# Shared expert blocks summed by twos, shorter scatters, and the last LayerNorm split over three engines, in a two-layer decoder

## The chip, the core and the metric

The kernel runs as one program on one core of a Trainium2 chip. The metric is the device time of a run in microseconds. Five engines work side by side, each in the order of its own queue: TensorE (PE in the profile), VectorE (DVE), ScalarE (ACT), GpSimd (POOL), and SyncE (SP), which here only issues transfers.

## The reference, cut to what matters

Two decoder layers over 512 tokens of 1024 columns, in float32. Each layer is a mixer and then a mixture of 64 experts:

```python
scores = sigmoid(xf @ router_w)
topi = top_k(masked(scores + router_b), 6)
for e, rows in experts:
    hb = silu(xf[rows] @ w_gate[e]) * (xf[rows] @ w_up[e])
    out[rows] += (hb @ w_down[e]) * topw[rows, e]
x = layer_norm(alpha * x + g2 * (out + shared(xf)))
```

Every token goes to 6 of 64 experts, 3072 rows in all, and every expert has 3 MB of weights (w_gate, w_up, w_down, 1 MB each). The second layer's last LayerNorm is the output.

## The kernel before, in words

The 512 tokens lie in four tiles of 128 (`self.x`). The router sorts the experts by their number of tokens, apart from the first two (SINGLE), and the sorted places are laid into **blocks** of 128 rows (`blocks`, L50): 20 lone blocks with one expert each, 14 two-expert blocks of 2 x 64 rows, 4 four-expert blocks of 4 x 32 rows. `share` (L1167) brings the capacities into the slot arithmetic; an expert with more rows than its place sends the rest through the loop in `extra` (L1683, loop at L1690), which stands behind the blocks and runs as many rounds as there are such parts.

`moe` (L1471) runs the 38 blocks (NB) in one loop from L1570. A round b works on three blocks. `widen` (L1327) multiplies block b with w_gate and w_up (L1336) and forms silu times up on ScalarE and VectorE (L1337, L1338). `narrow` (L1351) multiplies block b-1 with w_down (L1369), four experts in two halves with a yield between them. `turn` (L1316) transposes block b+1's gathered rows (L1324), `turn_back` (L1341) transposes block b's result (L1347), and `slots` makes the index lists of later blocks (L1270).

What happens to a block's result depends on its kind. A **lone** block is scaled on VectorE (L1375) and added to rows of a DRAM buffer `acc` by an indirect transfer of GpSimd (L1376), always 128 rows. A **shared** block is split into a high and a low part (yh, yl: L1383 to L1385) and brought back to the tiles by `combine` (L1390): for each of four tiles and two halves of the columns, two products with a one-hot matrix (L1396) into one PSUM buffer and one VectorE addition to `self.x` (L1397). These are eight units a block, four ahead of the next block's transposes and four behind them.

The order of TensorE's work in the loop is the program's (`manual_schedule`). SyncE issues the weight loads in order (L1302): gate and up go round five places (`eslot`, L1399), w_down round a ring of three (`slot`, L199), and the w_down of an expert is issued behind gate and up of the third expert after it (LAG). The PSUM buffers are three for products ("mm"), three for transposes and combines ("tr"), two small ones.

In the last round, `acc` is read back in eight pieces (L1615) and added on VectorE (L1616). Behind the loop the last block's combine and LayerNorm go tile by tile: two units, `ln_stats` (L307) with two statistics passes on VectorE, one aggregate and a root (L239 VectorE, L240 GpSimd), then `ln_next` (L318), two VectorE passes over 1024 columns. In the last layer tile 0 goes to ScalarE and GpSimd instead (`ln_here`, L327). There VectorE and GpSimd follow the order written in the program.

## Time and profile before

| | us |
|---|---|
| runs, median (three: 2149.96 to 2156.48) | 2151.9 |
| the profiled execution, its own time | 2150.13 |
| its span in the profile | 2148.1 |
| TensorE products busy in the span | 1955.6 |
| VectorE busy | 1236.2 |
| ScalarE busy | 508.3 |
| GpSimd busy | 441.2 |
| mean granted TensorE clock, as a share of full speed | 0.967 |

Busy times of engines overlap and don't add up to the span. A matmul's end is modelled, so what counts for TensorE is how far the starts of its instructions lie apart. "Idle before <- X" names what ended an engine's idle time; an engine with q behind it is that engine's instruction queue (waits, branches, issue of transfers).

### The profile page before, as it was taken

The numbers are of one execution on the slowest core, as the hardware profiler recorded it, in microseconds if no ns is written. First come the engines' busy times: TensorE is split into PE (matmuls) and PEld (weight loads), VectorE is DVE, ScalarE is ACT, GpSimd is POOL, SyncE is SP. The second block draws the span as 40 slices with busy tenths as digits, with TensorE's granted clock in tenths as the row PEclk, the third lists the DMA queues.
The fourth block names the chain that finished last, engine by engine and source line by source line (L and its number), as shares of the span: only waits on it lengthen the run. The fifth ranks groups of instructions, "written<-read, shape, count | busy, mean of one in ns | idle before, by whom it ended". The sixth has DMA issues, their size and how long they took to land. (4 is left out here: it accounts for less than half of the span.)

```text
span 2148.1 us, 28655 instructions
## 1 busy us (share of the span) xinstructions
PE 1955.6 (91%) x10619; PEld 1193.5 (56%) x10619; DVE 1236.2 (58%) x3169; ACT 508.3 (24%) x969; POOL 441.2 (21%) x313
## 2 busy tenths in 40 slices
PE   4999878999999999999688999999999999998995
PEld 3777778644443443443567877888443444443432
DVE  6666687844444553542778778578453535544436
ACT  3412533111111111111334455523111111111110
POOL 1222234111010110101034445144211010110102
PEclk9999998999999999999899999999999999999997
DMA  7765455998998989988332111128989989989893
GB/s 296 257 240 186 182 199 195 352 330 325 406 349 351 389 316 361 381 325 300 96 118 59 40 60 60 46 99 309 357 335 365 363 327 402 353 317 405 329 348 126
DMA packets 128679, 572.18 MB, mean 266 GB/s; under 512 B 16943, under 2 KB 54255, under 8 KB 72473
## 3 DMA queue, kind: packets, MB, share of 16 engines
q1 hardware_dynamic: 103600, 499.81, 60.1%
q0 software_dynamic: 19632, 55.79, 9.3%
q10 hardware_dynamic: 5304, 14.72, 1.9%
q8 instruction: 85, 1.39, 0.3%
q14 instruction: 58, 0.47, 0.1%
HBM read 550.33 MB, written 34.61 MB: 272 GB/s over the span
## 5 line engine op out<-in xcount | busy, mean ns | idle before, releaser
L1336 PE MATMUL ps_mm<-wslot,xT 128*64 128x512 f32 (+2 forms) x1216 | 404.5, 596 | 1.1 <-ACT xT L1325 0.8
L1369 PE MATMUL ps_mm<-wslot,hT 128*64 128x512 f32 (+2 forms) x1024 | 329.6, 627 | 20.1 <-DMA wslot<-in_moe_w_down_dram 19.9
L1338 DVE SCALAR_TENSOR_TENSOR hh<-hh,t,ps_mm 128x256 f32<-128x256 f32 x76 | 36.5, 480 | 434.5 <-ACT hh L1337 434.5
L1336 PE MATMUL ps_mm<-parts,xT 128*64 128x512 f32 (+2 forms) x832 | 280.0, 595 | 0.7 <-ACT xT L1325 0.4
L1336 PEld LDWEIGHTS ps_mm<-wslot,xT 128*64 128x64 f32 (+2 forms) x1216 | 142.1, 148 | 218.9 <-issue 205.7
L1369 PEld LDWEIGHTS ps_mm<-wslot,hT 128*64 128x64 f32 (+2 forms) x1024 | 105.5, 152 | 225.1 <-issue 197.5
L232 PE MATMUL ps_mm<-parts,hTh 128*128 128x256 f32 x704 | 206.7, 295 | 14.0 <-DVE op L400 6.9
L1294 POOL DMA_INDIRECT xg<-hd,idx x76 | 86.3, 1136 | 615.1 <-PE ps_tr L1396 525.4
L233 PE MATMUL ps_mm<-parts,hTh 128*128 128x256 f32 x704 | 204.0, 291 | 4.9 <-DVE parts L220 4.2
L234 PE MATMUL ps_mm<-parts,hTl 128*128 128x256 f32 x704 | 203.3, 291 | 0.0
L225 POOL TENSOR_TENSOR parts<-wslot,parts 128x512 fp32r<-128x512 f32 (+1 forms) x79 | 140.6, 1807 | 241.9 <-ACT parts L218 241.8
L1397 DVE TENSOR_TENSOR x<-x,ps_tr 128x512 f32<-128x512 f32 x288 | 183.6, 680 | 11.1 <-PE ps_tr L1396 10.4
L1337 ACT ACTIVATE hh<-ps_mm 128x256 f32<-128x256 f32 x76 | 29.2, 384 | 613.7 <-PE ps_mm L1336 613.7
L1376 POOL DMA_INDIRECT acc<-yh,row x40 | 64.8, 1620 | 498.9 <-DVE yh L1375 498.9
L1336 PEld LDWEIGHTS ps_mm<-parts,xT 128*64 128x64 f32 (+2 forms) x832 | 93.7, 144 | 130.5 <-issue 122.9
L1396 PE MATMUL ps_tr<-yh,ohs 128*128 128x512 f32 x288 | 137.4, 477 | 26.1 <-DVEq L1690 14.0
L232 PEld LDWEIGHTS ps_mm<-parts,hTh 128*128 128x128 f32 x704 | 137.3, 195 | 17.7 <-DVE op L400 4.6
L1325 ACT ACTIVATE xT<-ps_tr 128x512 f32<-128x512 f32 x152 | 84.0, 597 | 245.0 <-PE ps_tr L1324 245.0
L233 PEld LDWEIGHTS ps_mm<-parts,hTh 128*128 128x128 f32 x704 | 137.4, 195 | 6.8 <-DVE parts L220 4.8
L234 PEld LDWEIGHTS ps_mm<-parts,hTl 128*128 128x128 f32 x704 | 136.8, 195 | 2.2 <-issue 0.9
L234 PE MATMUL ps_mm<-hTh,parts 128*128 128x512 f32 (+1 forms) x296 | 120.6, 407 | 9.1 <-POOL parts L225 9.1
L232 PE MATMUL ps_mm<-hTh,parts 128*128 128x512 f32 (+1 forms) x296 | 123.7, 418 | 5.1 <-ACT parts L218 2.5
(456 smaller groups left out, 3124.3 us busy)
## 6 DMA issues: line engine op xcount, KB each, us to landing
wslot<-in_moe_w_down_dram SPq DMA_DIRECT2D x128, 1024.0 KB, 10.4
wslot<-in_moe_w_gate_dram SPq DMA_DIRECT2D x76, 1024.0 KB, 8.2
wslot<-in_moe_w_up_dram SPq DMA_DIRECT2D x76, 1024.0 KB, 11.7
parts<-in_moe_w_gate_dram SPq DMA_DIRECT2D x52, 1024.0 KB, 10.3
parts<-in_moe_w_up_dram SPq DMA_DIRECT2D x52, 1024.0 KB, 8.8
wslot<-in_ada_w_dram SPq DMA_DIRECT2D x44, 1024.0 KB, 5.6
wslot<-in_od_w_in_dram SPq DMA_DIRECT2D x16, 1024.0 KB, 6.2
wslot<-in_ev_w_in_dram SPq DMA_DIRECT2D x12, 1024.0 KB, 6.4
```

What stands on the lines that cost most here:

```text
L225: eng.tensor_sub(lo[:, ks], v[:, ks], hi[:, ks].bitcast(F32))
L232: self.nc.tensor.matmul(out, ah, bh, start=(i == 0), stop=False)
L233: self.nc.tensor.matmul(out, ah, bl, start=False, stop=False)
L234: self.nc.tensor.matmul(out, al, bh, start=False, stop=(i == n - 1))
L1294: self.nc.gpsimd.indirect_dma_start(out=xg, out_offset=None, in_=M["hd"], in_offset=bass.IndirectOffsetOnAxis(ap=idx, axis=0), bounds_chec ...
L1325: nc.scalar.activation(xT[:, 4 * g:4 * g + 4], pt.rearrange("p (k c) -> p k c", k=4), AF.Copy)
L1336: nc.tensor.matmul(pv[a:a + n], xT[:, i, a:a + n], w[0][:, :, i], start=(i == 0), stop=(i == KT - 1))
L1338: nc.vector.scalar_tensor_tensor(h, h, G["wt"], pg[:, FE:], op0=OP.mult, op1=OP.mult)
L1369: nc.tensor.matmul(py[a:a + n], hT[:, k, a:a + n], w[1][:, k, 512 * h:512 * h + 512], start=(k == 0), stop=(k == 1))
L1376: nc.gpsimd.indirect_dma_start(out=M["acc"], out_offset=bass.IndirectOffsetOnAxis(ap=G["tok"], axis=0), in_=yf, in_offset=None, bounds_che ...
L1396: nc.tensor.matmul(po, G["oh"][:, t], y[:, cs], start=(i + k == 0), stop=(i == len(Gs) - 1 and k == 1))
L1397: nc.vector.tensor_add(self.x[t][:, cs], self.x[t][:, cs], po)
```

## The change

Nine edits go together:

- `width`: lone places 9 to 13 get a capacity of 96 rows, 14 to 19 of 80 (128 before), and the scatter of L1376 carries only so many rows. The products keep 128 rows.
- `blocks`: lone and shared blocks are spread in another order; the last three blocks are a four-expert and two two-expert ones, where a lone one stood among them before.
- A lone block's scaled result has a buffer of its own (`ys`, one) and no longer shares the two of the shared blocks' high part; `hh` has one buffer in place of two.
- Shared blocks are combined by twos: the units of a pair make four products into one PSUM buffer and one addition. The last two shared blocks stay single.
- Behind a four-expert block the second half of `narrow` comes at the end of the round, behind the next transposes; the combine of a pair that ends with such a block comes a round later.
- `acc` is read into the three gather buffers, tiles 0 and 1 in round NB-3, 2 and 3 in round NB-2, and added on GpSimd a round later.
- LayerNorm behind the loop: the statistics of tiles 1 and 3 are made on ScalarE in two passes (`ln_stats_act`), one for the sum and one for the squares about the mean. This holds for both layers.
- In the last layer ScalarE and GpSimd also take the first half of tile 1's columns (`norm2`), and the order is written anew.
- In the first layer's output projection the closing step of a group of adaLN sums is no longer put off (`fill`).

```diff
@@ -47,6 +47,11 @@
 ALONE = SINGLE + FULL
 
 
+def width(k):
+
+    return P if k < SINGLE + 7 else 96 if k < SINGLE + 12 else 80
+
+
 def blocks():
 
 
@@ -62,10 +67,10 @@
         a, b = iter(out), iter(more)
         return [next(b if k in at else a) for k in range(n)]
 
-    alone = [((k, 0, P),) for k in range(ALONE)]
+    alone = [((k, 0, width(k)),) for k in range(ALONE)]
     twos = shared(ALONE, TWOS, 2)
     fours = shared(ALONE + TWOS, E - ALONE - TWOS, 4)
-    return alone[:SINGLE] + spread(spread(twos, fours), alone[SINGLE:], 0, 1)
+    return alone[:SINGLE] + spread(spread(twos, fours), alone[SINGLE:], 0.5, 3)
 
 
 BLOCKS = blocks()
@@ -314,6 +319,17 @@
         nc.vector.bn_aggr(mv[:, 0:2], st.rearrange("p a b -> p (a b)"))
         self.rsqrt(mv[:, 2:3], mv[:, 1:2], 1.0, LN_EPS)
         return mv
+
+    def ln_stats_act(self, x, scratch):
+
+        nc = self.nc
+        mv = self.small.tile([P, 4], F32, tag="mv", name="mv", bufs=4)
+        sm = self.small.tile([P, 3], F32, tag="lnsum", name="lnsum", bufs=2)
+        nc.scalar.activation(scratch, x, AF.Copy, accum_out=sm[:, 0:1])
+        nc.scalar.activation(sm[:, 2:3], sm[:, 0:1], AF.Copy, scale=-1.0 / D)
+        nc.scalar.activation(mv[:, 0:1], sm[:, 0:1], AF.Copy, scale=1.0 / D)
+        nc.scalar.activation(scratch, x, AF.Square, bias=sm[:, 2:3], accum_out=sm[:, 1:2])
+        return mv, lambda: self.rsqrt(mv[:, 2:3], sm[:, 1:2], 1.0 / D, LN_EPS)
 
     def ln_next(self, x, mv, rows, h):
 
@@ -1169,7 +1185,12 @@
         nc = self.nc
         cnt, posm = M["count"], M["posm"]
         of = {k: (a, n) for b in BLOCKS for k, a, n in b}
-        runs, k = [], ALONE
+        runs, k = [], SINGLE
+        for n in sorted({width(k) for k in range(SINGLE, ALONE)}, reverse=True):
+            m = sum(width(j) == n for j in range(SINGLE, ALONE))
+            if n < P:
+                runs.append((k, k + m))
+            k += m
         for n, m in ((TWOS, 2), (E - ALONE - TWOS, 4)):
             for j in range(m):
                 runs.append((k, k + n // m))
@@ -1329,7 +1350,7 @@
-        h = G["h"] = M["pool"].tile([P, FE], F32, tag="hh", name="hh", bufs=2)
+        h = G["h"] = M["pool"].tile([P, FE], F32, tag="hh", name="hh", bufs=1)
@@ -1351,9 +1372,9 @@
     def narrow(self, M, G):
 
         nc, hT, pool = self.nc, G["hT"], M["pool"]
-        one = G.get("one")
+        one = G.get("one", 0)
         if one:
-            (yh,) = [pool.tile([P, D], FR, tag="yh", name="yh", bufs=2)]
+            yf = pool.tile([P, D], F32, tag="ys", name="ys", bufs=1)
         elif "y" not in G:
             G["y"] = [pool.tile([P, D], FR, tag=n, name=n, bufs=2) for n in ("yh", "yl")]
             G["oh"] = pool.tile([P, TT, P], FR, tag="ohs", name="ohs", bufs=2)
@@ -1369,12 +1390,11 @@
         if one:
-            yf = yh.bitcast(F32)
             for h, py in enumerate(pys):
                 cs = slice(512 * h, 512 * h + 512)
                 nc.vector.tensor_mul(yf[:, cs], py, M["grow"][:, cs])
-            nc.gpsimd.indirect_dma_start(out=M["acc"], out_offset=bass.IndirectOffsetOnAxis(ap=G["tok"], axis=0),
-                                         in_=yf, in_offset=None, bounds_check=S + P - 1, compute_op=OP.add)
+            nc.gpsimd.indirect_dma_start(out=M["acc"], out_offset=bass.IndirectOffsetOnAxis(ap=G["tok"][:one], axis=0),
+                                         in_=yf[:one], in_offset=None, bounds_check=S + P - 1, compute_op=OP.add)
             yield
             return
         for h, py in enumerate(pys):
@@ -1509,7 +1529,7 @@
                 w = [[] for _ in es]
-                W.append([(a, n, x) for (_, a, n), x in zip(b, w)])
+                W.append([(a, n if len(b) > 1 else P, x) for (_, a, n), x in zip(b, w)])
@@ -1552,7 +1572,9 @@
         self.hes.close()
         with ExitStack() as es:
             M["pool"] = self.pool(f"exp{l}", ctx=es)
-            todo, units = [], []
+            todo, late, shared = [], [], 0
+            nshared = sum(len(b) > 1 for b in BLOCKS)
+            back = {NB - 3: ((), (0, 1)), NB - 2: ((0, 1), (2, 3)), NB - 1: ((2, 3), ())}
 
             for _ in range(NXG - SINGLE):
                 merge((slots(), 2))
@@ -1575,45 +1597,49 @@
                         row.append(self.narrow(M, G[b - 1]))
                         if not G[b - 1]["one"]:
                             todo.append(G[b - 1])
+                            shared += 1
                     if b < NB:
                         fetch(sum(2 * len(x) for x in BLOCKS[:b + LEAD]) + 2)
-                        G[b]["w"], G[b]["one"] = W[b], len(W[b]) == 1
+                        G[b]["w"], G[b]["one"] = W[b], len(W[b]) == 1 and BLOCKS[b][0][2]
                         row.append(self.widen(M, G[b]))
-                    if not todo:
+                    four = b > 0 and len(BLOCKS[b - 1]) > 2
+                    full = len(todo) == 2 or (todo and shared > nshared - 2)
+                    if not full and not four:
                         row.reverse()
                     for x in row:
                         next(x)
-                    for x in row:
+                    for x in row[four:]:
                         for _ in x:
                             pass
-                    if todo and b < NB:
-                        units = [lambda g=todo, t=t, h=h: self.combine(g, t, h) for t in range(TT) for h in range(2)]
+                    units, late = late, []
+                    if full and b < NB:
+                        late = [lambda g=todo, t=t, h=h: self.combine(g, t, h) for t in range(TT) for h in range(2)]
                         todo = []
+                        if not four:
+                            units, late = units + late, []
                     for u in units[:4]:
                         u()
                     if b + 1 < NB:
                         ahead()
-                    if b < NB and not units:
+                    if b < NB and not units and not four:
                         self.turn_back(M, G[b])
                     if b + 1 < NB:
                         self.turn(M, G[b + 1])
-                    if b < NB and units:
+                    if b < NB and (units or four):
                         self.turn_back(M, G[b])
                     next(sl, None)
                     for u in units[4:]:
                         u()
-                    units = []
                     if b == NB - 3 and pre:
                         pre(False)
                     if b == NB - 1 and pre:
                         pre(True)
-                    if b == NB - 1:
-                        for t in range(TT):
-                            for h in range(2):
-                                cs = slice(512 * h, 512 * h + 512)
-                                y = self.wk("acc")
-                                nc.gpsimd.dma_start(y, M["acc"][t * P:(t + 1) * P, cs])
-                                nc.vector.tensor_add(self.x[t][:, cs], self.x[t][:, cs], y)
+                    if NB - 3 <= b < NB:
+
+                        for t in back[b][0]:
+                            nc.gpsimd.tensor_add(self.x[t], self.x[t], M["xg"][(NB - 3 + t) % 3])
+                        for t in back[b][1]:
+                            nc.gpsimd.dma_start(M["xg"][(NB - 3 + t) % 3], M["acc"][t * P:(t + 1) * P])
                     if b == NB - 8:
                         wds = [wd[:, 1], wd[:, 0]]
                         new = lambda n: wds.pop()
@@ -1627,6 +1653,9 @@
                             nc.vector.tensor_mul(wd[:, k], wd[:, k], grow)
                     if 8 <= b < 24 and b % 2 == 0:
                         self.shared_end((b - 8) // 4, b // 2 % 2, parts, wd)
+                    for x in row[:four]:
+                        for _ in x:
+                            pass
             units = [lambda g=todo, t=t, h=h: self.combine(g, t, h) for t in range(TT) for h in range(2)]
             self.extra(M, l)
             M["h"], M["mv"] = M["xg"] + [M["tb"].bitcast(F32)], []
@@ -1635,33 +1664,75 @@
                 for u in units[2 * t:2 * t + 2]:
                     u()
 
+            mv, then = M["mv"], {}
+
             def stats(t):
-                M["mv"].append(self.ln_stats(self.x[t]))
-
-            mv = M["mv"]
+
+                if t % 2:
+                    m, then[t] = self.ln_stats_act(self.x[t], M["h"][t])
+                else:
+                    m = self.ln_stats(self.x[t])
+                mv.append(m)
 
             def store(t, cs):
                 nc.sync.dma_start(self.d["out"][0][t * P:(t + 1) * P, cs], self.x[t][:, cs])
 
+            def norm(t, cs=slice(0, D)):
+                to = M["h"] if nxt else self.x
+                self.ln_next(self.x[t][:, cs], mv[t], [r[:, cs] for r in M["rows"]], to[t][:, cs])
+                if not nxt:
+                    store(t, cs)
+
+            def norm2(t, cs):
+                x = self.x[t][:, cs]
+                nc.scalar.activation(x, x, AF.Identity, bias=mv[t][:, 3:4], scale=mv[t][:, 2:3])
+                yield
+                for op, r in zip((nc.gpsimd.tensor_mul, nc.gpsimd.tensor_add), M["rows"]):
+                    op(x, x, r[:, cs])
+                    yield
+                store(t, cs)
+                yield
+
+            lo, hi = slice(0, D // 2), slice(D // 2, D)
             with self.tc.manual_schedule(engines={mybir.EngineType.DVE, mybir.EngineType.Pool}):
-                for t in range(TT):
-                    sums(t)
-                    if nxt and t:
-                        self.ln_next(self.x[t - 1], mv[t - 1], M["rows"], M["h"][t - 1])
-                    stats(t)
-                    if not nxt and t == 0:
-                        self.ln_shift(mv[0])
-                        self.ln_here(self.x[0], mv[0], M["rows"], nc.gpsimd, nc.gpsimd)
-                        store(0, slice(0, D))
+                sums(0)
+                stats(0)
                 if nxt:
-                    self.ln_next(self.x[3], mv[3], M["rows"], M["h"][3])
+                    sums(1)
+                    stats(1)
+                    norm(0)
+                    then[1]()
+                    sums(2)
+                    norm(1)
+                    stats(2)
+                    sums(3)
+                    stats(3)
+                    norm(2)
+                    then[3]()
+                    norm(3)
                 else:
-                    for t in range(1, TT):
-                        x, n = self.x[t], D // 2 if t == 3 else D
-                        for k in range(0, D, n):
-                            cs = slice(k, k + n)
-                            self.ln_next(x[:, cs], mv[t], [r[:, cs] for r in M["rows"]], x[:, cs])
-                            store(t, cs)
+                    self.ln_shift(mv[0])
+                    g0, g1 = norm2(0, slice(0, D)), norm2(1, lo)
+                    next(g0)
+                    next(g0)
+                    sums(1)
+                    stats(1)
+                    sums(2)
+                    stats(2)
+                    next(g0)
+                    next(g0)
+                    sums(3)
+                    stats(3)
+                    then[1]()
+                    self.ln_shift(mv[1])
+                    next(g1)
+                    norm(2)
+                    then[3]()
+                    for _ in g1:
+                        pass
+                    norm(1, hi)
+                    norm(3, lo)
+                    norm(3, hi)
 
     def moe_end(self, l, xd, early, then):
 
@@ -1786,7 +1857,7 @@
 
             left = [0]
 
-            def fill(n=3):
+            def fill(n=3, wait=True):
 
                 n, left[0] = n + left[0], 0
                 for i in range(n):
@@ -1795,7 +1866,7 @@
                             return
                         l, g = todo.pop(0)
                         queue.extend(self.ada_slabs(l, g, t4, self.mod_end(l, g)))
-                    if i and len(queue) == 1:
+                    if wait and i and len(queue) == 1:
                         left[0] = n - i
                         return
                     queue.pop(0)()
@@ -1808,7 +1879,7 @@
             self.row(grow, self.mod[:, 0, 2])
             rows = self.rows_next(new, 0, 0, (self.mod[:, 0, 3], self.mod[:, 0, 4]))
             wr = self.router(0, new)
-            self.out_project(mixed, d["ev_w_out"][0], grow, d["x"][0], fill, (0, 1, 4, 5, 6, 7, 2, 3))
+            self.out_project(mixed, d["ev_w_out"][0], grow, d["x"][0], lambda: fill(3, False), (0, 1, 4, 5, 6, 7, 2, 3))
             while todo or queue:
                 fill(1)
             hT = self.moe_in(0, new, rows, wr)
```

## Rows read from the trace of the kernel before

**Rows 1.** The page, busy tenths of TensorE in 40 slices of 53.7 us.

```profile
PE   4999878999999999999688999999999999998995
```

**Rows 2.** Windows: stretch, us; busy us (instructions) of each engine, clock, DMA share, GB/s.

```profile
1496.00:2117.00 621.00, 597.30 (x2474) 269.35 (x2474) 287.98 (x850) 79.96 (x152) 80.37 (x63) 0.99 0.92 349
...
1650.00:1700.00 50.00, 49.14 (x212) 21.84 (x209) 26.21 (x84) 6.62 (x13) 6.69 (x6) 1.00 1.00 390
1850.00:1900.00 50.00, 49.18 (x199) 22.14 (x196) 24.12 (x75) 6.98 (x13) 6.39 (x5) 0.97 0.85 311
...
982.00:988.80 6.80, 5.99 (x14) 1.28 (x14) 0.69 (x1) 0.63 (x1) 0.00 (x0) 0.50 1.01 429
```

**Rows 3.** Waits of TensorE over the span: us in total, times, longest.

```profile
PE ps_mm L1369 <- DMA wslot<-in_moe_w_down_dram: 19.9, 8, 4.2
PE ps_tr L1396 <- DVEq L1690: 14.0, 2, 8.0
```

**Rows 4.** Timeline of TensorE, one combine in the second layer: start, us, what.

```profile
2037.45 0.79 PE L1396 MATMUL ps_tr<-yh,ohs 128*128 128x512 f32 x1
...
2040.20 1.31 PE L1324 MATMUL ps_tr<-call,xg 128*128 128x128 f32 x8
...
2041.78 0.47 PE L1396 MATMUL ps_tr<-yh,ohs 128*128 128x512 f32 x1
...
2042.33 0.39 PE L1396 MATMUL ps_tr<-yh,ohs 128*128 128x512 f32 x1
2042.56 0.40 PE L1396 MATMUL ps_tr<-yl,ohs 128*128 128x512 f32 x1
...
2043.93 0.62 PE L1336 MATMUL ps_mm<-wslot,xT 128*32 128x512 f32 x2
```

**Rows 5.** Lines by form, VectorE: count, busy us, mean ns, idle before.

```profile
L1397 DVE TENSOR_TENSOR x<-x,ps_tr 128x512 f32<-128x512 f32 x288 | 183.6, 680 | 11.1 <-PE ps_tr L1396 10.4
```

**Rows 6.** Timeline of TensorE, a combine behind a four-expert block and the products after it.

```profile
2078.87 0.50 PE L1396 MATMUL ps_tr<-yh,ohs 128*128 128x512 f32 x1
...
2082.39 1.31 PE L1324 MATMUL ps_tr<-call,xg 128*128 128x128 f32 x8
...
2086.03 7.09 PE L1336 MATMUL ps_mm<-wslot,xT 128*64 128x512 f32 x32
```

**Rows 7.** Waits of SyncE's queue over the span.

```profile
SPq L1302 <- PE ps_mm L1369: 237.8, 40, 12.5
```

**Rows 8.** Transfers: packets, MB, share of 16 engines; issues, us to landing.

```profile
q0 software_dynamic: 19632, 55.79, 9.3%
...
wslot<-in_moe_w_down_dram SPq DMA_DIRECT2D x128, 1024.0 KB, 10.4
...
acc<-yh,row POOLq DMA_INDIRECT x40, 10.8
```

**Rows 9.** Timeline of the second layer's hand-over.

```profile
2114.40 3.09 DVE L1616 TENSOR_TENSOR x<-x,acc 128x512 f32<-128x512 f32 x5
...
2121.26 0.68 DVE L1383 TENSOR_TENSOR y<-ps_mm,grow 128x512 f32<-128x512 f32 x1
...
2123.06 0.79 PE L1396 MATMUL ps_tr<-yh,ohs 128*128 128x512 f32 x1 [6.01 <-DVEq L1690]
```

**Rows 10.** Timeline of the last LayerNorm.

```profile
2125.96 1.28 DVE L312 BATCH_NORM_STATS2 bn<-x 128x6 f32<-128x512 f32 x2
...
2128.56 1.24 ACT L329 ACTIVATE x<-x,mv 128x1024 f32<-128x1024 f32 x1 [5.19 <-DVE mv L325]
...
2129.88 2.38 POOL L330 TENSOR_TENSOR x<-x,wd 128x1024 f32<-128x1024 f32 x1 [1.55 <-ACT x L329]
...
2144.37 0.75 DVE L322 SCALAR_TENSOR_TENSOR x<-x,mv,wd 128x512 f32<-128x512 f32 x1
```

**Rows 11.** Lines by form, ScalarE's read-out and GpSimd beside VectorE's LayerNorm.

```profile
L649 ACT ACTIVATION_READ_ACCUMULATOR sq<-mixed 128x1 f32 x48 | 9.4, 196 | 0.0
...
L1458 POOL TENSOR_TENSOR h<-h,lnrow 128x1024 f32<-128x1024 f32 x2 | 6.5, 3258 | 0.2
```

## The prediction

> **What bounds the kernel now.** I read the 40 slices first. TensorE's digits [rows 1] show two long plateaus of 8 and 9, slices 8 to 19 and 28 to 39: the expert loops of the two layers. The change touches these, the hand-over after each loop, and the last LayerNorm, so I asked for the stretches [rows 2]. The second layer's loop (1496 to 2117) keeps TensorE 597.3 us busy out of 621; the first layer's is like it. There is little idle time to remove there, so a gain has to come out of time that counts as busy. The transfers are nearly as full: 0.92 of the sixteen DMA engines over the loop, 1.00 in one 50 us stretch, 0.85 in another. Of the twelve such stretches from 1500 to 2100, four stand at 0.99 or more and the others between 0.85 and 0.94 (one of the full and the emptiest stand in the rows). So the loop has two limits a few per cent apart, TensorE first.
>
> The waits of TensorE [rows 3] name two that the change aims at: 19.9 us in eight waits for a w_down load, one per four-expert block, and 14.0 us in two waits at the loop of `extra` (L1690), one per layer.
>
> The timeline of one combine [rows 4] shows what the wait list hides. A product with the one-hot matrix follows the next after 0.23 us where nothing holds it (2042.33 to 2042.56). The eight of the first half take 2.75 us (2037.45 to 2040.20), the eight of the second 2.15 (2041.78 to 2043.93): 4.90 us for 16, where 16 x 0.23 is 3.68. Two products (0.46 us) feed one VectorE addition of 0.68 us [rows 5], and three PSUM buffers can't hide that: VectorE sets the pace. Behind a four-expert block it is worse, 3.52 us for the first half [rows 6], as it also waits for the evacuation just made.
>
> **The change, part by part.**
>
> *Shared blocks summed by twos.* Four products now feed one addition: 0.92 us of TensorE against 0.68 of VectorE, so TensorE sets the pace. A pair costs 32 x 0.23 = 7.4 us, some 7.6 with the starts, for two blocks. Of a layer's 18 shared blocks the first 16 go in pairs (12 two-expert, 4 four-expert ones), the last two singly as now. Before: 12 x 4.90 + 4 x 5.67 = 81.5 us; after: 8 x 7.6 = 60.8. That frees **20.7 us of TensorE per layer**. The 64 additions that go from each layer (43 us of VectorE) lie beside other work and count nothing by themselves.
>
> *The second half of a four-expert block's down product moves behind the transposes.* Its fourth w_down load can't start before the first half has freed a place in the ring of three. The move puts the next block's transposes, the turn back and the slot products in between, 1.6 us where they run now (2040.20 to 2041.78 [rows 4]), some 2 with the wait for the turned block's gate on VectorE. Eight waits of 2.5 us on average lose about 2 each: **7.5 us per layer**, 2.5 us left over. What is late next: this half now frees its own ring places 2 us later, and SyncE, which issues every weight load in order, already waits 237.8 us in 40 waits for exactly that line [rows 7]. So the w_down loads of the blocks behind a four start later.
>
> *What the transfers allow.* TensorE could go 28 us faster per layer, 2.3 us in each 50 us stretch. In the eight stretches with room it can have that (18.7 us); in the four full ones it can have only what the transfers give up. They give up something: the 20 scatters of a layer carry 128 rows now, and after the change 9 x 128 + 5 x 96 + 6 x 80 = 2112 instead of 2560. The software queue takes 9.3% of 2148 us [rows 8] for two layers of gathers (3072 rows each), scatters and 640 cleared rows: 200 us over 12544 rows, 16 ns a row, so 448 rows are 7.1 us per layer, 2.3 of them in the full stretches. Upper end: 21 us per layer. Lower end: nothing, if every us saved turns into a later weight wait, as the ring and the five gate/up places can't carry a lead from an empty stretch over to a full one. No row decides between the ends: the mean fill of 0.92 speaks for the upper one, SyncE's waits for ring places [rows 7] for the lower one. I take half: **10.5 us per layer, 21 for both**.
>
> *The order of lone and shared blocks.* Lone blocks bring 3 MB per 10 us of products, shared ones 6 MB per 10 us; the order changes from near-strict alternation to one with two pairs of neighbouring lone blocks, and ends four, two, two. The weights in total are the same. I cost it at nothing; its cover is the lead of the gate/up loads, and without it the two blocks behind a four pay, which is the third rival below. A lone block's result now has one buffer: the next lone block's multiplication must wait for the scatter, whose landing takes 10.8 us [rows 8]. Neighbouring lone blocks are about 12 us apart, so VectorE may wait a us or two, covered by the next block's gate and up products, 7.1 us [rows 6].
>
> *The read-back of the scattered rows* leaves VectorE. Before, its eight additions stand in VectorE's queue ahead of the last block's evacuation [rows 9]: after the last down products TensorE idles 6.01 us, until the combine starts at 2123.06. The multiplication at L1383 that ends this takes 0.68 us, and TensorE starts 1.1 us after it (2121.94 to 2123.06). Without the additions 1.8 us of the 6.0 are left: 4.2 gained; of the first layer's 8.0, 6.2. **10.4 us.** GpSimd now makes four additions of 1024 columns, 2.38 us each by its multiplication of that shape [rows 10]; the first two fall under the last blocks, the last two need the last combine of their tile and end beside the last down products and their evacuation. Cost zero to 2 us; zero taken, since tiles 2 and 3 are summed last.
>
> *The last LayerNorm.* VectorE runs nearly without gaps from the first addition to the end (2144.37 + 0.75). Two of four tiles lose their statistics there: two passes of 1.28 us together [rows 10], and some 0.3 for the aggregate and the root's first step (an estimate from two small steps behind a 1.28 us pair), so 2 x 1.6 = 3.2; half of tile 1 goes to ScalarE and GpSimd, 1.2 more. In exchange ScalarE takes 2 passes of 1.24 us (its pass over 1024 columns [rows 10]), two read-outs of 0.2 [rows 11] and two small ones per tile, 3.3 us. GpSimd is behind: its power for tile 1 waits for the second operation on tile 0, to about 2.3 us after VectorE wants it. Net 4.4 - 2.3 - 0.3 = 1.8. The first layer's version has no half tile and no such queue on GpSimd: 3.2 less 1.2 of waiting for ScalarE, 2. **Together 3.5 us.**
>
> Here a row speaks against the change: a GpSimd operation on 1024 columns took 2.38 us in the tail but 3.26 earlier [rows 11], while VectorE ran the two-operand LayerNorm passes. By this GpSimd's half tile costs 2.6 to 3.6 us and may end last, up to 1 us later than VectorE; that end is in the range. The Trainium skill, "SBUF — State Buffer", Who interferes with whom, says that a VectorE instruction with two SBUF inputs contends with a GpSimd instruction that reads SBUF. By that rule the tail gains about 0.8 us instead of 1.8; the rows agree with it in kind.
>
> *The rest:* the mod sums drawn into the output projection of layer 0 and two more groups in the capacity arithmetic are below 3 us either way; zero taken. The narrower capacities could send experts through `extra`; on the reference's own inputs the counts at the 10th and 15th place are 72 and 62 in the first layer, 81 and 72 in the second, under 96 and 80, so it stays at no rounds.
>
> **Sum:** 21 + 10.4 + 3.5 = 35 us off the profiled execution's 2150.1, that is 2115; the median of the runs stands 1.8 above it, so 2117.
>
> **The rivals.**
> 1. *TensorE gets all of its gain* (the transfers have room). For: the mean fill of 0.92. Against: four full stretches in twelve. 56 + 14 = 70 us off: 2082. The clock would add a little: behind the w_down wait at 982 the granted clock is 0.50 for 6.8 us [rows 2], the 1.2 GHz level, 3.4 us lost.
> 2. *The transfers are the bound at once*, and the loop keeps its length: 14 us off, 2138. For: 1.00 in the stretches that hold a four. Against: lower fill in eight of twelve.
> 3. *Slower, through the ring of three.* After a four, both halves hold ring places longer, and the w_down of the next two blocks is issued late; a load takes 10.4 us to land [rows 8], and 7.1 us of gate and up products [rows 6] cover it. That prices 3 to 8 us per four. It decides once a four loses over 8.7 us, as eight fours then eat the 70 us; with 10.4 us each, 13 us slower: 2165.
> 4. *No change*, the same mechanism at 8 to 9 us per four, 2152.
>
> **How the numbers follow.** The forecast 0.50, the first rival 0.17, the second 0.22, slower 0.06, no change 0.05. The range reaches from the first rival's side, 2081, to the second's plus the 3 us of unpriced edits, 2142. A measurement of this kernel tells about 0.3% (6.5 us) from no change. Forecast and first two rivals lie below 2145 but for 0.02 at the second's upper edge: faster 0.87, same 0.07, slower 0.06.
>
> **What would show it.** In the profile after: L1397 falls from 288 to 160 additions; 32 products of a pair in 7.4 to 7.7 us; the L1690 wait falls from 14.0 to about 4; the tail from the first addition to the end shrinks by under 2 us. TensorE's waits for w_down should move from the four itself to the blocks behind it, some 15 to 20 us per layer in all, with the DMA share at 0.95 or more. If these waits are under 5 us, the first rival holds; above 28 the second; L1397 waits unchanged would break the first step.

## The result and the profile after

The changed kernel takes 2172.8 us (median of four runs, 2170.77 to 2177.42) against 2150.9 for the kernel before beside it: ratio 1.0104, 95% interval 1.0074 to 1.0133. It is slower by 1%; 2117 was predicted. The profiled execution's span is 2168.8 us, 20.7 more than before.

Line numbers move: gate and up products are now L1357, down products L1390, the combine's products L1416 and additions L1417, the weight loads L1323.

The loops of the two layers, first gate product to last down product, took 625.2 and 620.6 us and take 636.8 and 634.2: 25.2 us more. The hand-overs behind them give back 4.0, a start 1.9 us earlier the same way, and what is left of the 20.7 is 1.3 us in the last LayerNorm and 0.1 elsewhere. So the loss is in the loops, where most of the gain was expected.

Waits of TensorE over the span, after (us in total, times, longest), beside [rows 3]:

```profile
PE ps_mm L1390 <- DMA wslot<-in_moe_w_down_dram: 56.2, 13, 9.4
...
PE ps_tr L1416 <- DVE x L1417: 10.7, 8, 3.5
PE ps_tr L1416 <- DVEq L1761: 9.9, 2, 5.0
```

The w_down waits grew from 19.9 us to 56.2. Of these, 36 us lie in the block two places behind a four, 15 in the block right behind the last four, 5 in the fours themselves. SyncE, which issues the loads, waits longer for the ring than in [rows 7]:

```profile
SPq L1323 <- PE ps_mm L1390: 311.7, 40, 15.5
```

This total alone does not tell a slow kernel from a fast one: in the order of early fours below it is 372.1 us, and the kernel is 75 us faster.

One of the long waits in the timeline of TensorE, in the two-expert block two places behind a four (its first two products, 1.04 us, then nothing):

```profile
1650.98 1.04 PE L1390 MATMUL ps_mm<-wslot,hT 128*64 128x512 f32 x2
1660.78 3.65 PE L1390 MATMUL ps_mm<-wslot,hT 128*64 128x512 f32 x8 [8.75 <-DMA wslot<-in_moe_w_down_dram]
```

Windows of the second layer after; columns as in [rows 2]. The whole loop; three rounds in which SyncE waits for a gate/up place; one round in which loads issued before keep the transfers full; the last 52.9 us cut where the layer's last weight packet lands; and the stretch around the wait above:

```profile
1502.90:2137.40 634.50, 594.63 (x2470) 280.51 (x2470) 254.35 (x780) 77.78 (x151) 84.76 (x63) 0.97 0.88 339
...
1683.60:1695.80 12.20, 11.99 (x56) 5.14 (x55) 4.28 (x14) 1.07 (x3) 0.45 (x1) 1.00 0.39 139
1838.10:1851.70 13.60, 13.60 (x59) 5.89 (x59) 5.95 (x24) 1.47 (x3) 1.55 (x2) 1.00 0.51 191
1900.70:1912.60 11.90, 11.69 (x40) 5.85 (x38) 4.89 (x17) 1.08 (x3) 0.46 (x1) 1.00 0.38 139
1991.90:2006.20 14.30, 14.01 (x65) 6.87 (x63) 7.87 (x30) 3.77 (x8) 0.11 (x1) 1.00 1.02 424
...
2084.50:2115.00 30.50, 22.91 (x90) 7.18 (x90) 7.05 (x8) 2.73 (x5) 6.93 (x6) 0.83 0.96 382
2115.00:2137.40 22.40, 21.41 (x88) 11.02 (x84) 15.63 (x26) 1.54 (x3) 3.65 (x2) 1.00 0.00 0
1654.00:1664.20 10.20, 3.42 (x8) 0.99 (x10) 0.00 (x0) 0.00 (x0) 0.00 (x0) 0.50 1.03 368
```

This is the reading that matters. **The transfers are not busier, they are worse spread.** In [rows 2] they were busy for 0.92 of 621 us, 571 us; now for 0.88 of 634.5, 558 us. They have less to do (the narrower scatters), yet they idle for 76 us where they idled for 50. Two kinds of places stand out, and the four rows that show them hold 44 of the 76 us. One is a round behind a pair sum or the second of two neighbouring lone blocks (139 to 191 GB/s, against 424 in the full round); the other is the whole of the last 22.4 us, when no weight is left to load and TensorE still has 22.4 us of products before it. What holds the loads in the first kind is a place for gate and up weights, 15.6, 13.4 and 17.4 us long. In the full round SyncE waits too, 15.5 us for a place in the ring, but enough loads are under way. Over 1900.7 to 1912.6 the longest wait of SyncE's queue is

```profile
SPq L1323 <- PE ps_mm L1357: 17.4, 1, 17.4
```

The last row of the windows shows what a wait for a weight costs besides: the granted clock is 0.50, the 1.2 GHz level, for 10.2 us. Such stretches grew from 27 to 44 us in the first layer's loop and from 14 to 41 in the second's.

The pair sums did come. Timeline of one pair: 16 products in 4.1 us, 16 more in 3.8, 7.9 us for two blocks where the forecast had 7.6:

```profile
1748.05 0.80 PE L1416 MATMUL ps_tr<-yh,ohs 128*128 128x512 f32 x1
...
1752.13 1.06 PE L1345 MATMUL ps_tr<-call,xg 128*128 128x128 f32 x8
...
1753.37 0.48 PE L1416 MATMUL ps_tr<-yh,ohs 128*128 128x512 f32 x1
...
1756.87 0.39 PE L1416 MATMUL ps_tr<-yl,ohs 128*128 128x512 f32 x1
1757.19 1.05 PE L1357 MATMUL ps_mm<-wslot,xT 128*32 128x512 f32 x4
```

And VectorE's additions by form, for [rows 5]:

```profile
L1417 DVE TENSOR_TENSOR x<-x,ps_tr 128x512 f32<-128x512 f32 x160 | 108.0, 686 | 31.2 <-PE ps_tr L1416 29.5
```

The hand-over of the second layer, for [rows 9], in the timeline:

```profile
2133.75 4.66 POOL L1640 TENSOR_TENSOR x<-x,xg 128x1024 f32<-128x1024 f32 x2 [28.79 <-DVE x L1417]
2134.78 3.92 DVE L1407 TENSOR_SCALAR ohs<-call,t 128x128 fp32r<-128x128 f32 x3
2138.62 0.68 DVE L1403 TENSOR_TENSOR y<-ps_mm,grow 128x512 f32<-128x512 f32 x1
2139.22 0.27 DVE L1407 TENSOR_SCALAR ohs<-call,t 128x128 fp32r<-128x128 f32 x1
...
2142.46 0.80 PE L1416 MATMUL ps_tr<-yh,ohs 128*128 128x512 f32 x1 [5.02 <-DVEq L1761]
```

Three one-hot tiles take 3.92 us beside GpSimd's two additions of 4.66; the fourth, alone, takes 0.27. So the evacuation that TensorE waits for starts some 3 us late, and the wait is 5.02 us where 1.8 was expected.

The last LayerNorm, for [rows 10]:

```profile
2156.13 0.55 POOL L245 TENSOR_TENSOR mv<-rs,mhalf 128x1 f32<-128x1 f32 x1
...
2156.71 0.16 DVE L341 SCALAR_TENSOR_TENSOR mv<-mv 128x1 f32<-128x1 f32 x1 [2.24 <-POOL mv L245]
...
2160.48 3.20 POOL L1691 TENSOR_TENSOR x<-x,wd 128x512 f32<-128x512 f32 x2
2160.81 1.75 DVE L337 SCALAR_TENSOR_TENSOR x<-x,mv,wd 128x512 f32<-128x512 f32 x1
2162.66 1.56 DVE L338 SCALAR_TENSOR_TENSOR x<-x,mv,wd 128x512 f32<-128x512 f32 x1
2164.15 0.74 DVE L337 SCALAR_TENSOR_TENSOR x<-x,mv,wd 128x512 f32<-128x512 f32 x1
```

### The profile page after: what moved, and what is told of

Read it like the earlier page. It is cut to its first block, busy times and chain, and to the rows that moved or that the text cites. A ratio compares the mean times of both kernels' runs of the same rounds, so it can differ in the third digit from the quotient of the medians.

```text
span 2168.8 us, 28521 instructions
## 1 busy us (share of the span) xinstructions
PE 1949.0 (90%) x10619; PEld 1217.4 (56%) x10619; DVE 1162.1 (54%) x3026; ACT 514.5 (24%) x994; POOL 461.1 (21%) x315
## 5 line engine op out<-in xcount | busy, mean ns | idle before, releaser
L1357 PE MATMUL ps_mm<-wslot,xT 128*64 128x512 f32 (+2 forms) x1216 | 407.6, 602 | 3.5 <-ACT xT L1346 2.4
L1390 PE MATMUL ps_mm<-wslot,hT 128*64 128x512 f32 (+2 forms) x1024 | 334.3, 625 | 56.3 <-DMA wslot<-in_moe_w_down_dram 56.2
L1357 PE MATMUL ps_mm<-parts,xT 128*64 128x512 f32 (+2 forms) x832 | 299.7, 600 | 1.1 <-ACT xT L1346 0.9
L1357 PEld LDWEIGHTS ps_mm<-wslot,xT 128*64 128x64 f32 (+2 forms) x1216 | 144.1, 148 | 209.8 <-issue 197.1
L1390 PEld LDWEIGHTS ps_mm<-wslot,hT 128*64 128x64 f32 (+2 forms) x1024 | 107.0, 152 | 263.1 <-issue 201.6
L237 PE MATMUL ps_mm<-parts,hTh 128*128 128x256 f32 x704 | 207.7, 296 | 12.8 <-DVE op L416 8.2
L1315 POOL DMA_INDIRECT xg<-hd,idx x76 | 92.9, 1222 | 526.6 <-PE ps_tr L1416 229.4
L1357 PEld LDWEIGHTS ps_mm<-parts,xT 128*64 128x64 f32 (+2 forms) x832 | 102.1, 148 | 131.3 <-issue 121.3
L1396 POOL DMA_INDIRECT acc<-ys,row x40 | 61.6, 1540 | 533.3 <-DVE ys L1395 533.3
L1416 PE MATMUL ps_tr<-yh,ohs 128*128 128x512 f32 x288 | 127.2, 443 | 20.8 <-DVE x L1417 10.7
L1417 DVE TENSOR_TENSOR x<-x,ps_tr 128x512 f32<-128x512 f32 x160 | 108.0, 686 | 31.2 <-PE ps_tr L1416 29.5
```

Of the source, the lines that this page charges most:

```text
L237: self.nc.tensor.matmul(out, ah, bh, start=(i == 0), stop=False)
L1315: self.nc.gpsimd.indirect_dma_start(out=xg, out_offset=None, in_=M["hd"], in_offset=bass.IndirectOffsetOnAxis(ap=idx, axis=0), bounds_chec ...
L1357: nc.tensor.matmul(pv[a:a + n], xT[:, i, a:a + n], w[0][:, :, i], start=(i == 0), stop=(i == KT - 1))
L1390: nc.tensor.matmul(py[a:a + n], hT[:, k, a:a + n], w[1][:, k, 512 * h:512 * h + 512], start=(k == 0), stop=(k == 1))
L1396: nc.gpsimd.indirect_dma_start(out=M["acc"], out_offset=bass.IndirectOffsetOnAxis(ap=G["tok"][:one], axis=0), in_=yf[:one], in_offset=None ...
L1416: nc.tensor.matmul(po, G["oh"][:, t], y[:, cs], start=(i + k == 0), stop=(i == len(Gs) - 1 and k == 1))
```

## The experiments

Each ratio is against the kernel before on the same chip, with its 95% interval.

**First four: which part costs it?** Theory R was my third rival, sharpened: the moved second half holds the ring. Theory F: TensorE got faster and the loads can't follow. Theory O: the order of the blocks.

*The second half stays* (edit on the changed kernel):

```diff
-                    for x in row[four:]:
+                    for x in row:
...
-                    for x in row[:four]:
-                        for _ in x:
-                            pass
```

> The changed kernel, but the second half of a four-expert block's down product runs where it ran before, straight behind the first half and the next block's gate and up products. Pair sums and everything else as changed. Theory R (the moved half holds its places in the ring of three a whole round longer): TensorE's waits for a w_down load fall from 56.2 us back to some 20 us, the stretches at half clock behind them go too (some 20 us), and the time is 2115 to 2140. Theory F (TensorE became faster through the pair sums and the loads can't follow; the place of the wait doesn't matter): the waits stay at 45 us or more and the time at 2160 to 2180.

Measured: 2173.2 us (1.0118, 1.0097 to 1.0140). No change. The w_down waits are 47.3 us in 15, the longest 6.9 instead of 9.4. Theory R falls for this kernel: the move sets where the wait stands, not how long the loop takes.

*Single sums*, the move kept:

```diff
-                    full = len(todo) == 2 or (todo and shared > nshared - 2)
+                    full = len(todo) > 0
```

> The changed kernel, but every shared block is summed by itself as before (two products to an addition), the moved second half kept. Theory R: the waits for w_down stay at 40 us or more, the pair sums' gain of 11 to 14 us a layer is lost on top, 2180 to 2200. Theory F: the waits fall to 25 us or less and the time to 2140 to 2160.

Measured: 2188.9 us (1.0194, 1.0171 to 1.0217), waits 47.5 us in 14. These are theory R's numbers, and theory F's are missed: the pair sums do not make the waits.

*Both undone:*

> The changed kernel with both undone: single sums, and a four-expert block's second half where it was. What is left of the change is the order of blocks, the narrower scatters, the read-back on GpSimd and the last LayerNorm. Theories R and F both: waits for w_down about 20 us, 2135 to 2150. Theory O (the new order of lone and shared blocks is the cause): waits of 35 us or more and 2160 or above here too.

Measured: 2170.4 us (1.0101, 1.0070 to 1.0131), waits 32.4 us in 13. With both accused parts gone the kernel is as slow as with them. So what is left (order, read-back, scatters, LayerNorm, and the small edits) holds the loss. One piece of the move is still in: here, and wherever only the second half goes back, a four's sum comes a round later. The single buffers of the lone blocks are in too; no run takes them back, but in the changed kernel's trace VectorE waits for one only 6.1 us in four waits. Between these two runs the move costs 18.5 us under single sums, and under pair sums nothing: the two parts do not add up, and neither theory R nor theory F says why.

*The order half a step earlier, its heavy end kept:*

```diff
-    return alone[:SINGLE] + spread(spread(twos, fours), alone[SINGLE:], 0.5, 3)
+    return alone[:SINGLE] + spread(spread(twos, fours), alone[SINGLE:], 0, 3)
```

> The changed kernel with the first lone block at the start of the alternation, as before, instead of half a step in (the end with three shared blocks kept). Theory O: waits for w_down fall to 25 us, 2120 to 2140. Theories R and F: within 8 us of the changed kernel's 2172.8, waits 45 to 60 us.

Measured: 2180.9 us (1.0150, 1.0118 to 1.0183), waits 56.7 us. The half step is not the cause; the last argument, which keeps lone blocks out of the last three places and crowds them into neighbours before, was still in.

**The old order.** Theory E, new here, is theory O narrowed down: the loads of the order's heavy end come late. *The kernel before with the new order alone* (`spread(…, 0.5, 3)` in it):

> The kernel before with one edit: the new order of blocks (lone blocks half a step later, and a four and two two-expert blocks at the end instead of four, lone, two, two). Theory E (the order's heavy end: with no lone block among the last three, and two pairs of neighbouring lone blocks in the middle that leave the transfers idle, the loads of the last 48 MB... that is of a four and two twos come late): the last rounds of each layer get some 11 to 14 us longer, 2165 to 2180. Theory R (the moved second half and the pair sums are the cause, which are not in this kernel): within 5 us of before's 2148.

Measured: 2160.0 us (1.0047, 1.0029 to 1.0066). Slower by 10, less than expected, and the w_down waits are before's (20.1 us): so the order costs little on its own.

*The changed kernel with the old order*, `spread(…, 0, 1)`, and, as a lone block's scatter now comes later, the old read-back:

```diff
-                    if NB - 3 <= b < NB:
...
+                    if b == NB - 1:
+                        for t in range(TT):
+                            for h in range(2):
+                                cs = slice(512 * h, 512 * h + 512)
+                                y = self.wk("acc")
+                                nc.gpsimd.dma_start(y, M["acc"][t * P:(t + 1) * P, cs])
+                                nc.vector.tensor_add(self.x[t][:, cs], self.x[t][:, cs], y)
```

> The changed kernel with the old order of blocks and, as the order allows no other, the old read-back of the scattered rows on VectorE. Pair sums, moved second half, narrower scatters, single buffers and the last LayerNorm as changed. Theory E: 2110 to 2138 (pair sums 11 to 14 us a layer less some waits for w_down). Theory R: waits for w_down at 50 us or more, 2150 to 2175.

Measured: 2135.4 us (0.9920, 0.9892 to 0.9949): 37 us below the changed kernel, and faster than the kernel before. The time is theory E's; the w_down waits are still 37.3 us.

*The same with the second half where it was:*

> As the run with the old order, and the second half of a four-expert block's down product where it was before. Theory E with a ring that the move holds longer: 5 to 15 us below that run, 2105 to 2130, the longest w_down wait below 5 us. Theory E alone: within 5 us of that run. Theory R: 2145 or above only if the pair sums do nothing.

Measured: 2137.7 us (0.9927, 0.9899 to 0.9955). Again the move is worth nothing.

*The same with the rows added on GpSimd in halves, in the last round:*

```diff
+                        for t in range(TT):
+                            for h in range(2):
+                                cs = slice(512 * h, 512 * h + 512)
+                                nc.gpsimd.tensor_add(self.x[t][:, cs], self.x[t][:, cs], got[t, h])
```

> As the run before this one (old order, second half stays), but the scattered rows are read back in the last round and added on GpSimd, eight additions of 512 columns that run while the last block's down product and its evacuation run. If taking the additions off VectorE is worth what was predicted (10.4 us for both layers): 8 to 11 us below that run. If GpSimd's additions hold up VectorE's one-hot tiles, as the three of 3.93 us in the changed kernel suggest: 0 to 4 us below.

Measured: 2132.2 us (0.9903, 0.9877 to 0.9928); the wait ahead of the last combine falls from 15.1 to 8.9 us, but the intervals overlap: unclear here.

**Smaller terms, and another order.** *Statistics of tiles 1 and 3 on VectorE again:*

```diff
-                if t % 2:
-                    m, then[t] = self.ln_stats_act(self.x[t], M["h"][t])
-                else:
-                    m = self.ln_stats(self.x[t])
+                m, then[t] = self.ln_stats(self.x[t]), lambda: None
```

> The changed kernel with the statistics of tiles 1 and 3 back on VectorE, in both layers, everything else as changed. If ScalarE's two passes are worth what was predicted (3.5 us for both layers), this run is 3 to 5 us slower than the changed kernel's 2172.8. If the passes on ScalarE only move the work to an engine that ends as late (the tail from the first product of the last combine to the end took 25.0 us before and 26.3 after), it is within 2 us, and that tail stays between 25 and 28 us.

Measured: 2175.2 us (1.0120, 1.0100 to 1.0141). From the last combine's first product (2145.22 in its timeline) to the end of the span (2172.3) it takes 27.1 us; in the changed kernel 26.3 (2142.46 to 2168.8).

*The changed kernel with the old read-back:*

> The changed kernel with the old read-back of the scattered rows: eight additions on VectorE in the last round; the new order of blocks stays. If the read-back on GpSimd gains the predicted 10.4 us: 2180 to 2185. If it gains only the 2 to 4 us that the wait ahead of the last combine shows (9.9 us for both layers against 14.0): 2174 to 2178. If GpSimd's additions cost elsewhere as much as they gain: 2168 to 2173.

Measured: 2174.2 us (1.0111, 1.0085 to 1.0137). The read-back on GpSimd gained 1.4 us, within the scatter.

*Old order, 128 rows in every scatter* (`width` returns P):

> The changed kernel with the old order of blocks and the old read-back (2135.4 us in its run), and with 128 rows in every scatter instead of 128, 96 and 80. If the transfers feel the 448 rows of 16 ns a layer: 3 to 12 us slower, 2138 to 2148. If the places for the weights set the pace and not the transfers' sum: within 3 us.

Measured: 2147.3 us (0.9993, 0.9978 to 1.0008) against 2135.4 with narrow ones: the narrower scatters are worth 12 us, 16 by the two ratios. So nearly all that the old order gains over the kernel before is theirs: its two loops are together about 13 us shorter than before's, and with 128 rows about 3.

*Early fours.* The same 38 blocks, ordered so that a four has lone blocks on both sides. The expectation below says that neighbouring two-expert blocks are summed together. This is not so: pairs are made in the order in which shared blocks come, so of two neighbours the first ends one pair and the second begins the next (the last two are summed singly):

```diff
-    return alone[:SINGLE] + spread(spread(twos, fours), alone[SINGLE:], 0.5, 3)
+    kinds = {1: iter(alone), 2: iter(twos), 4: iter(fours)}
+    return [next(kinds[int(m)]) for m in "11214121141112122141112112212212214122"]
```

> The changed kernel with the old read-back and another order of the same 38 blocks: the four-expert blocks early and with lone blocks on both sides, two-expert blocks in neighbouring couples that are summed together (sizes 1 1 2 1 4 1 2 1 1 4 1 1 1 2 1 2 2 1 4 1 1 1 2 1 1 2 2 1 2 2 1 2 2 1 4 1 2 2). If the order of the loads' sizes against the eight places that hold them is what costs (theory E): 2100 to 2130, and w_down waits below the 37.3 us of the run with the old order. If any order does as well: within 5 us of 2135. If only the end matters, which is the old one here: 2130 to 2140.

Measured: 2097.3 us (0.9751, 0.9726 to 0.9777), 75 us below the changed kernel with the same instructions but for the read-back. Waits of TensorE (lines are one higher here), and windows of the first layer's loop, whole and cut where its last weight packet lands:

```profile
PE ps_tr L1417 <- DVEq L1763: 15.8, 2, 8.3
...
PE ps_mm L1391 <- DMA wslot<-in_moe_w_down_dram: 5.2, 4, 2.8
```

```profile
402.50:996.80 594.30, 580.89 (x2470) 281.85 (x2470) 252.70 (x783) 79.58 (x152) 69.87 (x60) 0.99 0.94 363
402.50:978.30 575.80, 563.25 (x2392) 274.84 (x2394) 240.80 (x761) 76.13 (x148) 67.02 (x55) 0.99 0.97 372
978.30:996.80 18.50, 17.64 (x80) 7.01 (x76) 11.90 (x23) 3.44 (x4) 2.85 (x5) 1.00 0.25 81
```

The transfers are busy for the same 559 us (0.94 of 594.3) and idle for 36; until the last weight has landed they stand at 0.97.

**How order, pairs and move hang together.** *The kernel before with early fours alone:*

> The kernel before with one edit, the order of blocks of the run with early fours. If the order by itself decides how well the eight places stay filled: 2115 to 2135, w_down waits well under before's 19.9 us. If it is worth something only together with the pair sums: within 6 us of before's 2149.

Measured: 2149.2 us (0.9998, 0.9984 to 1.0011). Nothing, in either direction: with TensorE's work as it was, the order of early fours brings no time by itself.

*The last four shared blocks of a layer at once*, with the second half where it was (against the first run, 2173.2):

```diff
-                    full = len(todo) == 2 or (todo and shared > nshared - 2)
+                    full = len(todo) == 2 or (todo and shared > nshared - 4)
...
-                        if not four:
+                        if not four or shared > nshared - 4:
```

> The changed kernel with the second half where it was (2173.2 in its run) and the last four shared blocks of a layer summed singly and in their own round, so that 32 products and not 64 are left when the last weight load of the layer has landed. If those products are lost time, as nothing is left to load beside them: 7.4 us a layer less, 2157 to 2167. If TensorE only waits as much longer for the last loads: 2170 to 2176.

Measured: 2153.8 us (1.0015, 1.0002 to 1.0027): 19.4 us less, more than expected. Windows of its second layer around the last weight packet:

```profile
2076.90:2106.30 29.40, 24.90 (x107) 9.41 (x107) 12.83 (x22) 4.04 (x7) 6.99 (x6) 1.00 1.00 396
2106.30:2119.10 12.80, 12.60 (x54) 5.19 (x50) 6.28 (x11) 0.99 (x2) 3.41 (x2) 1.00 0.00 2
```

Behind the last packet 12.8 us of loop are left instead of the 22.4 of the changed kernel; the first layer goes from 24.9 to 14.3.

*Early fours with the second half where it was:*

> The changed kernel with early fours and the old read-back (2097.3), and the second half of a four-expert block's down product where it was before. If the move saves what was predicted where no other load is late (7.5 us a layer): 2108 to 2114. If the ring hides it: within 4 us of 2097.

Measured: 2118.0 us (0.9856, 0.9833 to 0.9879). Here the move is worth 20.7 us.

*Early fours with single sums:*

> The changed kernel with early fours and the old read-back (2097.3), and every shared block summed by itself. If the pair sums are worth the predicted 20.7 us a layer: 2133 to 2142. If they are worth the 12 to 15 us that the combine lost in the trace (82 us a layer before, 68 to 71 after): 2119 to 2129. If the loads give the pace in this order too: under 2105.

Measured: 2115.7 us (0.9834, 0.9813 to 0.9854). Here the pairs are worth 18.4 us.

**Two small terms where loads are hardly late.** *Early fours, rows added on GpSimd in halves:*

> The changed kernel with early fours (2097.3 with the read-back on VectorE), the scattered rows read back in the last round and added on GpSimd in eight additions of 512 columns. If the additions ahead of the last evacuation cost what was predicted (10.4 us for both layers): 2085 to 2090, and the wait ahead of the last combine falls from 15.8 us to about 4. If GpSimd ends its additions as late as VectorE came free: 2092 to 2099, and that wait stays above 8 us.

Measured: 2088.9 us (0.9710, 0.9696 to 0.9724), with the next run the fastest of the study. The wait ahead of the last combine:

```profile
PE ps_tr L1417 <- POOL x L1648: 8.9, 2, 5.2
```

*Early fours, statistics on VectorE:*

> The changed kernel with early fours and the read-back on VectorE (2097.3), with the statistics of tiles 1 and 3 back on VectorE in both layers. If ScalarE's passes are worth the predicted 3.5 us: 2099 to 2103. If they are worth nothing: 2095 to 2099.

Measured: 2088.9 us (0.9726, 0.9706 to 0.9746), not slower than with ScalarE's passes (0.9751, 0.9726 to 0.9777). It also equals the run before this one, on the same chip, with the read-back still on VectorE: so the 8.4 us between 2097.3 and 2088.9, which were measured on two chips, cannot be put down to the read-back. Its last LayerNorm takes 25.9 us from the combine's first product, the other's 25.2.

## Why the prediction was wrong

| us, median | neither | move alone | pairs alone | both |
|---|---|---|---|---|
| changed order | 2170.4 | 2188.9 | 2173.2 | 2172.8 |
| old order | 2149 (before) | | 2137.7 | 2135.4 |
| early fours | 2149.2 (before but for the order) | 2115.7 | 2118.0 | 2097.3 |

"Neither" in the old order and in early fours is the kernel before: it lacks the narrower scatters (12 us) and the other edits too, so in these two rows only the other columns can be compared with each other. In the changed order a four's sum still comes a round later under "neither" and "pairs alone".

And the first layer's loop, cut at its last weight packet (the second layers are within 4 us of it). Of the products left, 16 stand behind the loop in every row:

| | to the last packet | behind it | combine products left at it |
|---|---|---|---|
| before | 608.5 | 16.8 | 32 |
| before, new order | 612.6 | 15.0 | 32 |
| changed, neither | 615.5 | 20.8 | 48 |
| changed, pairs alone | 609.4 | 25.3 | 64 |
| changed | 611.9 | 24.9 | 64 |
| changed, old order and read-back | 600.9 | 17.1 | 32 |
| last four at once | 611.9 | 14.3 | 32 |
| early fours | 575.8 | 18.5 | 32 |

**The step that failed is the order, "I cost it at nothing".** "The weights in total are the same" is true and beside the point: eight places hold the weights, and a load can start only when products free one. In the changed order the last packet lands 609 to 616 us after the start of the first layer's loop, whether TensorE sums in pairs or not (626 with the move under single sums). What the pairs save comes back as waiting, with half clock behind it. The same edits reach 575.8 in the order of early fours. The forecast named a cover for this step and its price without it (the third rival), but gave it no term in the sum; with the old order the changed kernel runs at 2135.4, so the order took 37 us, or 39 if the old read-back that goes with it costs the 1.4 of its own run. By the traces of the two, 26 us of it lie ahead of the last packet (11 and 15 in the two layers) and 12 behind it (8 and 4). On the kernel before the same order cost 10: the rest is what the order takes from the other edits.

**"What the transfers allow" failed in its sign.** The forecast took half of TensorE's 28 us a layer, between a mean fill of 0.92 as room and its own lower end, nothing; the loops lost 12.6 us a layer, beyond that end. The fill is no stock to draw on: idle transfers in a round that waits for places (0.38 to 0.51) are not made up in a later one, which is full already (1.02). The working that would have served is transfers' own time plus the time they must idle: 558 + 76 us now, 559 + 36 with early fours. That is bookkeeping after the fact; the idle time would have had to be worked out round by round from the order.

**A term was missing: what is left when the last weight has landed.** A pair sum that is put off to the second block, and a four's sum put off by a round, leave 64 combine products instead of 32 behind it, 8.1 us of loop more in the first layer and 6.2 in the second (24.9 for 16.8, 22.4 for 16.2). The run with the last four at once takes them out: 11.0 and 8.8 us go behind the last packet, 2.5 and 2.0 are lost ahead of it, and 19.4 go in all, the rest in the hand-overs and outside the loops. The 14.3 us are more than half of the 25.2 by which the loops grew; the other 3.4 and 7.5 lie ahead of the last packet.

*Pair sums:* 7.9 us a pair against 7.6, right in the trace. By the starts of TensorE's products the combine took 87 and 86 us in the two layers' loops and takes 73 and 71, 14 to 16 less where 20.7 were counted, in part because the last 32 products of a loop take 12.3 and 10.1 us. Worth 18.4 us of the whole time where loads keep up, against 41 counted; there the combine itself is 31 us shorter than with single sums.

*The move:* 15 us forecast for both layers; 20.7 with early fours, nothing in the old and the changed order, and 18.5 lost in the changed order with single sums. The waits went where the forecast said, to the blocks behind a four, but with 28 us a layer instead of 15 to 20. By the forecast's own sign (above 28) that speaks for the second rival, but its 2138 is 35 us off. The share of the transfers, which was to be 0.95 or more, is 0.88: that sign spoke against the whole working.

*Narrower scatters:* 14.2 us of transfer time for both layers counted, 12 measured. Right.

*Read-back:* 10.4 us forecast; the wait fell by 4.1 (14.0 to 9.9) and the time by 1.4. That the last additions "end beside the last down products and their evacuation. Cost zero to 2 us" is the step: they hold up the one-hot tiles by 3 us. The Trainium skill, "SBUF — State Buffer", Who interferes with whom, says that a one-input VectorE operation of this kind can take the port pair that GpSimd uses, and that the second to come is blocked until the first ends; by that the tiles wait out the additions. The trace agrees: the three end at 2138.70, 0.3 us after the additions, and take 3.92 us instead of three times 0.27. In smaller pieces and with early fours the wait fell by 6.9 us (15.8 to 8.9). Whether the time follows is not shown: the run with both small terms on VectorE has the same 2088.9, and in the old order the intervals overlap.

*LayerNorm:* 3.5 us forecast, 1.8 of it in the last one. That one got 1.3 us longer (25.0 to 26.3 from the combine's first product), so not even the 0.8 us of gain came that the forecast worked out from the row against it and set aside. The statistics on ScalarE gain a little: 0.8 us in the changed kernel (26.3 for 27.1) and 0.7 with early fours (25.2 for 25.9). The step that failed is the half tile, "1.2 more": with it and VectorE's statistics the last LayerNorm takes 27.1 us, 2.1 more than before. VectorE's passes beside GpSimd's half tile take 1.75 and 1.56 us instead of 0.74, 1.8 us lost; no run takes the half tile back alone. The 2.24 us wait for GpSimd's power came as forecast (2.3). On the whole time no gain can be told.

Of the rivals the third had the sign and the place of the longest waits, at a chance of 0.06, and 2165 for 2172.8. Its cause was not the move, which it blamed (without it 2173.2), but the order under it, so its near number is luck.

## What to carry to other kernels

Where a few buffers feed a loop, the order of large and small blocks is part of the cost: for each stretch compare what it frees with what can be loaded, and for the end count the work left when the last load has landed. Here a saving on the busy engine was worth next to nothing until the order let the loads use it, and an order that was worth nothing alone (2149.2) was worth 38 us under it (2135.4 to 2097.3). The mean fill of the transfers says how much work they have, not how much room.

## What was not expected of the hardware

Loads of 1 MB kept the transfers at 424 GB/s over 14.3 us (the window from 1991.90), where the loop's mean is 339. And around the wait of 8.75 us the granted clock stood at 0.50 for 10.2 us (1654.0 to 1664.2), from within the wait to 3.4 us into the products behind it.
